# The casts of the activations' fourth combination, kept behind the last early Silu on ScalarE

## The chip, the cores and the metric

The kernel runs on one core of one Trainium2 chip. A core has five engines with an instruction queue each: TensorE (PE in the profile; its weight loads are shown as PEld), VectorE (DVE), ScalarE (ACT), GpSimd (POOL) and SyncE (SP), whose queue here issues most transfers to the 16 DMA engines. Every engine runs its queue in order, and the queues wait for each other. The metric is the device time of one execution in microseconds (us).

## The reference

The reference is a trunk of two layers on 1024 tokens of width 1024, in float32. A layer is a token mixer (latent attention in the first, differential attention in the second) and a SwiGLU feed-forward block, each followed by a layer norm on the residual sum. The change lies in the feed-forward block:

```python
D_FF = -(-8 * D_MODEL // (3 * 256)) * 256        # 2816

def _swiglu(x, w_gu, w_down):
    gate, up = jnp.split(x @ w_gu, 2, axis=-1)
    return (jax.nn.silu(gate) * up) @ w_down
...
        h = _layernorm(ALPHA * h + mix, ln_mix_g[i], ln_mix_b[i])
        h = _layernorm(ALPHA * h + _swiglu(h, ffn_w_gu[i], ffn_w_down[i]), ln_ffn_g[i], ln_ffn_b[i])
```

## The kernel before, in words

**Products.** Every float32 operand is split into a high part, a cast to fp32r on ScalarE (`A.copy`, in the profile CAST), and a low part, the rest, subtracted on VectorE or GpSimd. A product is three matmuls: high by high, high by low, low by high. The helper `split` (line 521) does this for all operands, so L521 stands for casts and low parts of many tiles; the tile's name tells them apart (t4h and t4l are the high and low part of t4; op_g and op_gp are split weights).

**The feed-forward block** (function `ffn`, called once per layer; I call the calls the first and the second block). The hidden width is 22 columns of 128, handled in the order `order`, n = 0 to 21. The two matmuls of gate and up with x are done by a Strassen-like scheme on 2 x 2 blocks: seven products per n instead of eight, named "1" to "7". Products "1" and "2" use the activations as they are (xh, xl) and accumulate into a bank `ga`; "5" and "3" use the combinations t1 and b22 and accumulate into `gc`; "6", "7" and "4" use t2, t3 and t4 and accumulate into `gb`. A product in the up-projection is twelve matmuls at line 565. The combinations of the activations are sums and differences of four blocks r11, r12, r21, r22 (tile xr), made in place on VectorE (lines 738 and 759) and split by `part`. The fourth combination, t4, is r21 - r22, with r22 already replaced by the second combination; its four casts write the tile t4h, four subtractions t4l.

**Early gates.** For n = 0 to 5 (`npre` = 6) products "1" and "2" are done ahead, while the last rows of the mixer are still on their way (`gates(0)`, `gates(2)`, `gates(4)`, two columns each). ScalarE copies the first result to the tile pg (line 626) and applies Silu to the second (line 628), into the same tile. `gates(2)` and `gates(4)` then store pg to HBM (line 704, tile pg_dr), as the buffer is wanted: all tiles made by `big_tile` share five buffers, and the raw weights gr of a later column, loaded at line 574, go where pg was. pg_dr is loaded back into tmp when n comes up (line 671).

**The main stream.** `stream` lists the products in the order of use, and `prepare` makes the weights' combinations (lines 596, 600, 602 and 606 on VectorE, on the tile gr) and splits them four products ahead. `consume` issues the twelve matmuls and then reads the bank on VectorE: after "6" at line 648, after "7" at line 652, after "4" at line 659. As "6", "7" and "4" of one n share a bank, the matmuls of "7" wait for line 648 and those of "4" for line 652. Two banks are there for gb, and TensorE takes n = 0 and n = 1 in turns.

**Order of work.** The order on each engine is written at build time by the tile framework's scheduler, from program order, priorities and modelled times. What the author wants otherwise is fixed by hand: `behind(i, j)` keeps instruction i behind instruction j; on one engine this is an order in its queue, with no semaphore. `part` takes such instructions as `after`, the first for the cast, the second for the low part. `newest` is a dictionary that remembers the latest instruction of some kind.

```python
        def part(key, k, src, eng, after=()):
            for i, j in zip(split([t[:, k] for t in xs[key]], src[:, k], eng), after):
                behind(i, j)
...
        gates(4)
...
        second("t3", r11, r22, r11, V, held)
        for k in range(4):
            part("t4", k, r21, V)
```

Of the kernel before, what the change touches and what calls it, by code (L numbers as in the profile page):

```python
# [11 lines left out]
AF = mybir.ActivationFunctionType  # L12
# [30 lines left out]
def trunk(  # L43
# [33 lines left out]
    V, A, G, T = nc.vector, nc.scalar, nc.gpsimd, nc.tensor  # L77
# [36 lines left out]
    def ps_s(name):  # L114
        return ps.tile([P, 512], F32, tag="s", bufs=ps_bufs[0], name=name)

    def ps_m(name):
        return ps.tile([P, 512], F32, tag="m", bufs=ps_bufs[1], name=name)
# [17 lines left out]
    newest = {}  # L136
# [43 lines left out]
    def behind(i, j):  # L180

        tc.add_manual_dep(
            i, j.name,
            mybir.DependencyInfo(mybir.DependencyClass.NoSync, mybir.DependencyReason.DATA),
            reason="kept in program order",
        )
# [162 lines left out]
    class OutProj:  # L349
# [73 lines left out]
        def split(self, tb, hs, o):  # L423
            oh, ol = (t[:, hs] for t in self.oh[tb])
            i = A.activation(oh, o, AF.Copy, scale=self.scale)
            j = V.scalar_tensor_tensor(ol, o, self.scale, f32(oh), ALU.mult, ALU.subtract)
            if tb in LAST_ORDER[2:4] and hs.start == 0:
                behind(i.ins, newest["hi"])
                behind(j.ins, newest["lo"])
# [107 lines left out]
    def ffn(side, xo, xst, pending, layer, x_src, x_dst, lng, lnb, next_x):  # L537
# [14 lines left out]
        r, tmp, ops, acc, hp, pg = {}, {}, {}, {}, {}, {}  # L552
        pg_dr = dr.tile([npre // 2, P, 4, 512], F32, name=f"pg_dr{layer}")

        def p1g0(n):


            t, i = (tmp[n], 2) if n in tmp and n > 1 else (pg[n // 2], 2 * (n % 2))
            return t[:, i], t[:, i + 1]

        def product(o, w, x, first):
            for k in range(4):
                kc = slice(k * P, (k + 1) * P)
                for a, b in ((0, 0), (0, 1), (1, 0)):
                    T.matmul(  # L565
                        o, w[:, a, kc], x[b][:, k, :], start=(first and k == 0 and (a, b) == (0, 0)),
                        stop=(k == 3 and a == 1), skip_group_check=True,
                    )
# [45 lines left out]
        def consume(n, pr):  # L614


            w, nm_ = ops.pop((n, pr)), f"{layer}_{n}"
            if pr in "12":
                if pr == "1":
                    acc[n, "a"] = ps_s(f"ga{nm_}")  # L620
                    if n >= npre:
                        new_tmp(n)
                product(acc[n, "a"], w, xo["12".index(pr), 0], pr == "1")
                p1, g0 = p1g0(n)
                if pr == "1":
                    A.copy(p1, acc[n, "a"])
                else:
                    A.activation(g0, acc[n, "a"], AF.Silu)
                return
            if pr in "53":  # L630
                if pr == "5" or n < 2:
                    acc[n, "c"] = c = (ps_s if n == 1 else ps_t)(f"gc{nm_}{pr}")
                    acc.setdefault((n, "cs"), []).append(c)
                product(acc[n, "c"], w, xs["t1" if pr == "5" else "b22"], pr == "5" or n < 2)
                if n < 2:
                    return
            else:
                if pr == "6":
                    acc[n, "b"] = ps_m(f"gb{nm_}")
                    if n < npre:  # L640
                        new_tmp(n)
                product(acc[n, "b"], w, xs[{"6": "t2", "7": "t3", "4": "t4"}[pr]], pr == "6")
            u2, u3 = tmp[n][:, 0], tmp[n][:, 1]
            p1, g0 = p1g0(n)
            if n == NFF - 1 and pr in "57":
                V.tensor_tensor(u3, p1 if pr == "5" else u3, acc[n, "c" if pr == "5" else "b"], ALU.add)
            elif pr == "6":
                V.tensor_tensor(u2, p1, acc[n, "b"], ALU.add)
                for c in acc[n, "cs"] if n < 2 else ():
                    V.tensor_tensor(u2, u2, c, ALU.add)  # L650
            elif pr == "7":
                V.tensor_tensor(u3, p1, acc[n, "b"], ALU.add)  # L652
                if n < 2:
                    V.tensor_tensor(u3, u3, acc[n, "cs"][0], ALU.add)
            elif pr == "5":
                V.tensor_tensor(u3, u3, acc[n, "c"], ALU.add)
            elif pr == "4":
                if n < NFF - 1:
                    V.tensor_tensor(p1, p1, acc[n, "b"], ALU.add)
            else:  # L660
                V.tensor_tensor(u2, u2, acc[n, "c"], ALU.add)  # L661
            if pr == ("4" if n < 2 else "3") and n < NFF - 1:
                activations(n, u2, u3, p1, g0)

        def new_tmp(n):
            if n == NFF - 1:
                tmp[n] = big_tile(f"tmp{layer}_{n}", F32).rearrange("p a (b c) -> p (a b) c", b=2)
                return
            tmp[n] = pool_a.tile([P, 4, 512], F32, tag="ra", name=f"tmp{layer}_{n}", bufs=2)
            if 1 < n < npre:  # L670
                nc.sync.dma_start(tmp[n][:, 2:4], pg_dr[n // 2][:, 2 * (n % 2):2 * (n % 2) + 2])

        def activations(n, u2, u3, p1, g0, after=()):
            j, kh = n // 2, n % 2
            i = A.activation(u2, u2, AF.Silu).ins  # L675
            for k in after[:1]:
                behind(i, k)
            if n == NFF - 1:
                i = V.tensor_tensor(p1, p1, acc[n, "b"], ALU.add).ins
                behind(i, after[1])  # L680
            if kh == 0:
                hp[j] = big_tile(f"hp{layer}_{j}", F32).rearrange("p a (b c) -> p (a b) c", b=2)

            i = V.tensor_tensor(hp[j][:, kh], g0, p1, ALU.mult).ins
            for k in after[1:]:
                behind(i, k)
            V.tensor_tensor(hp[j][:, 3 - kh], u2, u3, ALU.mult)
            if kh:
                h11, h12, h22, h21 = (hp[j][:, i] for i in range(4))
                t = big_tile(f"sh{layer}_{j}", F32).rearrange("p a (b c) -> p (a b) c", b=2)  # L690
                G.tensor_tensor(t[:, 0], h21, h22, ALU.add)
                G.tensor_tensor(t[:, 1], t[:, 0], h11, ALU.subtract)
                G.tensor_tensor(t[:, 2], h11, h21, ALU.subtract)
                G.tensor_tensor(t[:, 3], h12, t[:, 1], ALU.subtract)
                d = h_dr[j // 4][:, :, j % 4, :].rearrange("s p c -> p s c")
                nc.sync.dma_start(d[:, 0:3], hp[j][:, 0:3])
                nc.sync.dma_start(d[:, 3:7], t)

        def gates(n):
            for pr in "12":  # L700
                for i in (n, n + 1):
                    consume(i, pr)
            if n:
                nc.sync.dma_start(pg_dr[n // 2], pg[n // 2])
# [13 lines left out]
        r11, r12, r21, r22 = (xo["r", k, t] for k, t in ((0, 0), (0, 1), (1, 0), (1, 1)))  # L718
# [6 lines left out]
# [3 lines that stand above are left out]
# [31 lines left out]
            V.tensor_tensor(r21[:, k], r21[:, k], r22[:, k], ALU.subtract)  # L759
        second("t3", r11, r22, r11, V, held)  # L760
        for k in range(4):
            part("t4", k, r21, V)
        for i, u in enumerate(stream):
            if i + ahead < len(stream):
                prepare(*stream[i + ahead])
            consume(*u)
# [609 lines left out]
    xo, stacks = x_pools("m0", "right")  # L1376
    pending = out_proj("left", w_o_a, o_dr[0], x, xs_dr[0], ln_mix_g[0], ln_mix_b[0], xo)
    xT, rest, normed = ffn("left", xo, stacks, pending, 0, xs_dr[0], xs_dr[1], ln_ffn_g[0], ln_ffn_b[0], next_x)


# [186 lines left out]
    pending = proj[0].rest(ln_mix_g[1], ln_mix_b[1], xo)  # L1567
    banks("ps4", PS_BUFS)
    ffn("right", xo, stacks, pending, 1, xs_dr[2], out, ln_ffn_g[1], ln_ffn_b[1], None)
    ps_stack.close()  # L1570

# [87 lines left out]
```

## Time and profile before

| what | value |
|---|---|
| device time, median of 3 runs | 2265.44 us (2265.01 to 2267.45) |
| span of the profiled execution, first to last instruction | 2269.7 us |
| TensorE busy | 2238.7 us (99% of the span), 10850 matmuls |
| VectorE busy | 1593.1 us (70%) |
| ScalarE busy | 1007.1 us (44%) |
| GpSimd busy | 886.3 us (39%) |
| granted TensorE clock, mean | 0.997 of full speed |
| transfers | 289.25 MB, 127 GB/s on average |

How to read it: the profile is one execution, taken by the hardware profiler. Its span is 4.3 us longer than the median of the timed runs; no other time is given for the profiled execution, so differences are worked out on the span and taken over to the median. A busy engine is one with an instruction under way. The granted clock is the share of full speed that TensorE was given. The first feed-forward block's up-projections run from about 447 us to 868 us of the span, the second's from about 1626 us to 2052 us.

### The profile page before, as it was taken

How to read it: one execution, taken by the hardware profiler on the slowest of the kernel's cores; microseconds unless marked ns; L12 is line 12 of the kernel's file. 1: busy time of each engine (PE TensorE's matmuls, PEld its weight loads, DVE VectorE, ACT ScalarE, POOL GpSimd, SP SyncE). 2: the span in 40 equal slices, each digit the busy share in tenths (PEclk: the TensorE clock that was granted, in tenths of full speed). 3: DMA queues.
4: the chain of work that ended last, by engine and by line, in shares of the span. 5: the costliest groups of instructions: out<-in, count | busy, mean ns of one | idle time of the engine just before them, and what ended most of it. 6: DMA issues, size and time to landing. Idle time of an engine off the chain costs nothing.

```text
span 2269.7 us, 30075 instructions
## 1 busy us (share of the span) xinstructions
PE 2238.7 (99%) x10850; PEld 1883.5 (83%) x10850; DVE 1593.1 (70%) x2944; ACT 1007.1 (44%) x2077; POOL 886.3 (39%) x711
## 2 busy tenths in 40 slices
PE   9999999999999999999999999999999999999998
PEld 9888897878888888887888888877778888888886
DVE  6677774596656667778578777676586666568778
ACT  4455563352333334445466656555442332334444
POOL 2243451104544445555333435321014444446552
PEclk9999999999999999999999999999999999999999
DMA  6121335334324138454311212153334323247544
GB/s 207 41 95 59 121 98 186 116 145 148 139 70 139 70 114 335 177 199 153 112 43 33 61 35 64 42 209 114 137 132 150 108 83 126 82 150 269 204 171 159
DMA packets 104420, 289.25 MB, mean 127 GB/s; under 512 B 8656, under 2 KB 32080, under 8 KB 93776
## 3 DMA queue, kind: packets, MB, share of 16 engines
q1 hardware_dynamic: 100272, 277.90, 35.0%
q0 software_dynamic: 4000, 9.44, 1.5%
q8 instruction: 85, 1.39, 0.2%
q14 instruction: 63, 0.52, 0.1%
HBM read 205.78 MB, written 77.33 MB: 125 GB/s over the span
## 4 chain that ended last, share of the span: by engine, by line
PE 46%; DVE 5%; issue 1%; DMA 1%; ACT 1%; POOL 1%; POOLq 0%; DVEq 0%; SPq 0%; ACTq 0%
PE gb L565 8%; PE gc L565 5%; PE dw L871 4%; PE ga L565 4%; PE zp_a L440 3%; PE dx L871 3%; PE s_b L239 3%; PE bp L168 2%; PE bp L170 2%; PE bp L169 2%; PE bv L1409 2%; PE dv L871 1%; PE dy L871 1%; PE o_b L274 1%; PE pt_b L173 1%
## 5 line engine op out<-in xcount | busy, mean ns | idle before, releaser
L521 ACT CAST op_g<-gr 128x512 fp32r<-128x512 f32 x240 | 147.5, 622 | 403.5 <-PE gb L565 225.4
L521 POOL TENSOR_TENSOR op_g<-gr,op_g 128x512 fp32r<-128x512 f32 x104 | 146.1, 1410 | 303.4 <-DVE tmp L661 160.0
L521 DVE TENSOR_TENSOR op_h<-rh,op_h 128x512 fp32r<-128x512 f32 x154 | 164.0, 1090 | 58.8 <-ACT op_h L521 58.7
L565 PE MATMUL ga<-xh_m,op_g 128*128 128x512 f32 x512 | 168.0, 389 | 0.0
L871 PE MATMUL dw<-op_w_t,op_h 128*128 128x512 f32 x660 | 153.1, 391 | 1.8 <-DVE op_h L521 1.8
L521 ACT CAST op_h<-rh 128x512 fp32r<-128x512 f32 x154 | 92.3, 619 | 139.9 <-DMA rh<-h_dr 42.8
L871 PEld LDWEIGHTS dw<-op_w_t,op_h 128*128 128x128 f32 x660 | 123.2, 188 | 28.3 <-DVE op_h L521 2.8
L245 ACT ACTIVATE l_b<-l_b,mx_b 128x256 f32<-128x256 f32 (+7 forms) x128 | 99.5, 777 | 73.5 <-DVE mx_b L242 70.4
L521 POOL TENSOR_TENSOR op_w_t<-tt,op_w_t 128x512 fp32r<-128x512 f32 x66 | 98.2, 1490 | 81.2 <-ACT op_w_t L521 81.2
L565 PE MATMUL gb<-t3h_f,op_g 128*128 128x512 f32 x352 | 117.0, 394 | 3.6 <-ACT tmp L675 2.9
L1462 POOL TENSOR_SCALAR l_b<-l_b,r_b,cst 128x128 f32<-128x128 f32 (+3 forms) x64 | 52.5, 821 | 174.2 <-DVE r_b L247 152.9
L871 PE MATMUL dx<-op_w_b,op_h 128*128 128x512 f32 x528 | 120.3, 389 | 0.0
L565 PE MATMUL gb<-t4h_f,op_g 128*128 128x512 f32 x352 | 115.7, 390 | 0.8 <-DVE tmp L652 0.8
L871 PEld LDWEIGHTS dx<-op_w_b,op_h 128*128 128x128 f32 x528 | 99.1, 188 | 20.6
L521 DVE TENSOR_TENSOR op_g<-gr,op_g 128x512 fp32r<-128x512 f32 x136 | 110.3, 811 | 8.4 <-ACT op_g L521 8.1
L565 PE MATMUL gc<-b22h_f,op_g 128*128 128x512 f32 x352 | 115.5, 389 | 0.0
L565 PE MATMUL gc<-t1h_f,op_g 128*128 128x512 f32 x352 | 115.5, 389 | 0.0
L565 PE MATMUL gb<-t2h_f,op_g 128*128 128x512 f32 x352 | 115.1, 389 | 0.0
L521 POOL TENSOR_TENSOR op_g<-s,op_g 128x512 fp32r<-128x512 f32 x40 | 54.3, 1358 | 151.8 <-ACT op_g L521 151.7
L565 PEld LDWEIGHTS ga<-xh_m,op_g 128*128 128x128 f32 x512 | 96.1, 188 | 19.9
L168 PE MATMUL bp<-xT_f,h_wb 128*128 128x512 f32 x256 | 103.2, 403 | 0.2
L169 PE MATMUL bp<-xT_f,h_wb 128*128 128x512 f32 x256 | 101.9, 398 | 0.0
(389 smaller groups left out, 6567.9 us busy)
## 6 DMA issues: line engine op xcount, KB each, us to landing
gr<-in_w_gu SPq DMA_DIRECT2D x44, 1024.0 KB, 6.9
rh<-h_dr SPq DMA_DIRECT2D x28, 1024.0 KB, 5.0
h_dr<-sh SPq DMA_DIRECT2D x22, 1024.0 KB, 4.9
h_dr<-hp SPq DMA_DIRECT2D x22, 768.0 KB, 4.0
tt<-in_w_dn SPq DMA_DIRECT2D x22, 512.0 KB, 8.2
rh<-h_dr SPq DMA_DIRECT2D x14, 768.0 KB, 4.4
z<-xs_dr SPq DMA_DIRECT2D x16, 512.0 KB, 11.3
rw_b<-in_w_dn SPq DMA_DIRECT2D x8, 1024.0 KB, 8.1
```

What stands on the lines that cost most here:

```text
L168: T.matmul(ps_out, lh, rh, start=(i == 0), stop=False)
L169: T.matmul(ps_out, lh, rl, start=False, stop=False)
L170: T.matmul(ps_out, ll, rh, start=False, stop=(i == n - 1))
L173: T.transpose(ps_out, in_, ident)
L239: T.matmul(s[:, :w], lh, rh[:, ks], start=(j == 0), stop=(j == len(q_pass) - 1))
L245: newest["exp"] = A.activation(l[:, :n], l[:, :n], AF.Exp, bias=mx, scale=-1.0, accum_out=sm).ins
L440: T.matmul(m, a[:, h, :], self.wo[h][w][:, c], start=(start and h == heads[0] and a is oh and w == 0), stop=(stop and h == heads[-1] and a ...
L521: return A.copy(hi, src).ins, eng.tensor_tensor(lo, src, f32(hi), ALU.subtract).ins
L565: T.matmul(o, w[:, a, kc], x[b][:, k, :], start=(first and k == 0 and (a, b) == (0, 0)), stop=(k == 3 and a == 1), skip_group_check=True,)
L871: i = T.matmul(o, h[:, a, c], w[:, b_], start=(first and (a, b_) == (0, 0)), stop=(last and a == 1), skip_group_check=True,).ins
L1409: T.matmul(m, xT[0][hf][:, k, c], w[k], start=(k == 0), stop=False, skip_group_check=True)
L1462: G.tensor_scalar(l1[:, :n], l1[:, :n], r1, nlam, ALU.mult, ALU.mult)
```

## The change

In `consume` the Silu of every early or later gate is remembered as `newest["silu"]`. Where the fourth combination is split, the four casts on ScalarE are kept behind the Silu that is the newest at that point. At that point in the program the last Silu issued is the one in `gates(4)`, for n = 5. The low parts on VectorE get no order of their own (`after` has one entry). The same code runs in both blocks.

```diff
@@ -625,7 +625,7 @@
                 if pr == "1":
                     A.copy(p1, acc[n, "a"])
                 else:
-                    A.activation(g0, acc[n, "a"], AF.Silu)
+                    newest["silu"] = A.activation(g0, acc[n, "a"], AF.Silu).ins
                 return
             if pr in "53":
                 if pr == "5" or n < 2:
@@ -759,7 +759,7 @@
             V.tensor_tensor(r21[:, k], r21[:, k], r22[:, k], ALU.subtract)
         second("t3", r11, r22, r11, V, held)
         for k in range(4):
-            part("t4", k, r21, V)
+            part("t4", k, r21, V, (newest["silu"],))
         for i, u in enumerate(stream):
             if i + ahead < len(stream):
                 prepare(*stream[i + ahead])
```

## Rows read from the trace of the kernel before

**Rows 1.** The page: part 1, busy us by engine; part 4, the chain's shares
```profile
PE 2238.7 (99%) x10850; PEld 1883.5 (83%) x10850; DVE 1593.1 (70%) x2944; ACT 1007.1 (44%) x2077; POOL 886.3 (39%) x711
...
PE 46%; DVE 5%; issue 1%; DMA 1%; ACT 1%; POOL 1%; POOLq 0%; DVEq 0%; SPq 0%; ACTq 0%
```

**Rows 2.** Waits of TensorE, whole span: total us, times, longest us
```profile
PE gb L565 <- ACT tmp L675: 2.9, 1, 2.9
...
PE gb L565 <- DVE tmp L652: 0.8, 1, 0.8
...
PE gb L565 <- ACT op_g L521: 0.7, 1, 0.7
```

**Rows 3.** The chain in order of time, second block: start us, us, what
```profile
1668.51 4.09 DMA pg_dr<-pg
...
1672.66 6.18 DMA gr<-in_w_gu
...
1678.93 0.69 DVE gr L596
```

**Rows 4.** Stretches: length, busy us by engine (instructions), PEclk, DMA share, GB/s
```profile
500.10:503.00 2.90, 2.90 (x12) 2.12 (x12) 2.90 (x4) 0.63 (x1) 1.29 (x1) 1.00 0.00 0
1664.00:1666.00 2.00, 2.00 (x11) 1.65 (x10) 2.00 (x4) 0.20 (x1) 0.00 (x0) 1.00 0.00 0
1668.00:1670.00 2.00, 2.00 (x11) 1.65 (x10) 2.00 (x5) 2.00 (x4) 0.00 (x0) 1.00 0.97 410
1682.70:1687.20 4.50, 4.43 (x13) 3.53 (x14) 4.19 (x6) 1.12 (x2) 1.28 (x1) 0.62 0.00 0
```

**Rows 5.** Timeline of TensorE, second block: start us, us, line, what, [idle before]
```profile
1663.18 0.39 PE L565 MATMUL ga<-xh_m,op_gp 128*128 128x512 f32 x1
...
1671.34 0.39 PE L565 MATMUL gb<-t2h_f,op_g 128*128 128x512 f32 x1
...
1682.77 0.47 PE L565 MATMUL gb<-t3h_f,op_g 128*128 128x512 f32 x1 [2.93 <-ACT tmp L675]
...
1687.18 0.40 PE L565 MATMUL gb<-t4h_f,op_g 128*128 128x512 f32 x1
...
1689.92 0.39 PE L565 MATMUL gc<-t1h_f,op_g 128*128 128x512 f32 x1
```

**Rows 6.** Timeline of VectorE, second block
```profile
1676.05 0.68 DVE L648 TENSOR_TENSOR tmp<-pg,gb 128x512 f32<-128x512 f32 x1
1678.93 0.69 DVE L596 TENSOR_TENSOR gr<-gr 128x512 f32<-128x512 f32 x1 [2.20 <-DMA gr<-in_w_gu]
...
1681.95 0.67 DVE L648 TENSOR_TENSOR tmp<-pg,gb 128x512 f32<-128x512 f32 x1
...
1685.02 0.67 DVE L652 TENSOR_TENSOR tmp<-pg,gb 128x512 f32<-128x512 f32 x1
```

**Rows 7.** Timeline of ScalarE, first block
```profile
483.12 0.60 ACT L628 ACTIVATE pg<-ga 128x512 f32<-128x512 f32 x1 [1.59 <-PE ga L565]
...
484.61 2.19 ACT L521 CAST t4h_f<-xr_m 128x512 fp32r<-128x512 f32 x4 [0.37 <-DVE t3l_f L521]
```

**Rows 8.** Timeline of ScalarE, second block
```profile
1665.81 2.19 ACT L521 CAST t4h_f<-xr_m 128x512 fp32r<-128x512 f32 x4 [2.75 <-DVE t3l_f L521]
1667.90 0.58 ACT L628 ACTIVATE pg<-ga 128x512 f32<-128x512 f32 x1
```

**Rows 9.** Waits of SP's queue, 1655 to 1675 us
```profile
SPq L704 <- ACT pg L628: 2.9, 1, 2.9
```

**Rows 10.** Timeline of SP's queue, 1664 to 1668 us
```profile
1665.20 0.33 SPq L574 DMA_DIRECT2D gr<-in_w_gu  x1
```

**Rows 11.** The tile gr, 1650 to 1690 us: its loads, from issue to landing
```profile
DMA to landing us min/median/max: 4.8/4.9/6.2
```

**Rows 12.** Timeline of TensorE, first block
```profile
491.08 0.39 PE L565 MATMUL gb<-t2h_f,op_g 128*128 128x512 f32 x1
...
503.83 0.50 PE L565 MATMUL gb<-t4h_f,op_g 128*128 128x512 f32 x1 [0.76 <-DVE tmp L652]
```

## The prediction, made before the changed kernel was run

> **What bounds the kernel now.** I read the page first: TensorE is busy for 99% of the span, and the chain that ended last is TensorE where it is not short bits of VectorE, ScalarE and transfers [rows 1]. So an edit that adds no matmul can only give back or take TensorE's waits. I then listed those waits over the whole execution: the up-projections (gb) lose 2.9 us once, 0.8 us once and 0.7 us once [rows 2]. The 2.9 us lie in the second feed-forward block, the two small ones in the first, as the timelines show. Next I followed the chain back from the 2.93 us. It reads, backwards: a matmul at 1682.77, VectorE's add on gr at 1678.93, the load of gr issued at 1672.66, the store of pg at 1668.51, which waits for pg [rows 3]. What writes pg is the Silu of the last early gate, n = 5, on ScalarE. The load of raw weights for n = 4 (I call it gr4) goes into the buffer that the stored gates leave, so it can't be issued before the store has landed.
>
> The table of stretches shows a second loss at the same place: behind the wait the granted clock averages 0.62 from 1682.7 to 1687.2, so part of it ran at 1.2 instead of 2.4 GHz [rows 4]. The twelve matmuls of that product stretch from 1682.77 to 1687.18, 4.41 us; the next twelve, at full clock, stretch from 1687.18 to 1689.92, 2.74 us [rows 5]. The clock costs 1.67 us; wait and clock together cost 2.93 + 1.67 = 4.60 us. That is the most that the change can give back there, 0.20% of the time.
>
> One name in the waits is not the true one. The profile puts the 2.93 us down to a Silu on tmp. The product needs the bank that VectorE's L648 reads, at 1681.95 for 0.67 us [rows 6]: its end, 1682.62, is 0.15 us ahead of the matmul. So TensorE starts again at the end of L648 plus 0.15 us.
>
> **The change part by part.** Nothing is computed anew and no semaphore is added: `behind` only fixes an order on one engine. In the first block the Silu of n = 5 starts at 483.12 and the four casts t4h at 484.61 [rows 7]; the order asked for is already there, and I cost the edit at nothing. In the second block the casts start at 1665.81 and the Silu at 1667.90 [rows 8]; here they change places.
>
> What the Silu gains. Its last matmul starts at 1663.18 and takes 0.39 us, so its input stands at 1663.57 [rows 5]. ScalarE is idle for the 2.75 us ahead of 1665.81, so from 1663.06, for the casts wait for a VectorE result [rows 8]. The Silu (0.58 us) fits into that gap, over by about 1664.2 instead of 1668.48, and the casts still start at 1665.81: putting them behind costs nothing as long as VectorE is what they wait for. If that cover were gone they would be late by at most the Silu's 0.58 us, with their first reader on TensorE at 1687.18.
>
> What the store gains. It doesn't go at 1664.2: the queue of SP has a gr load at 1665.20 ahead of it, and from there the store waited 2.9 us for the Silu [rows 9, 10]. With the Silu early it follows the load's issue of 0.33 us, at about 1665.6 instead of 1668.51. Landing: before, it took 4.1 us (1668.51 to 1672.6) [rows 3]; alone it would land at 1669.7. But it now lies wholly beside the gr load of 1665.20. Two transfers of 1 MB are 2.1 MB; at the 410 GB/s that the DMA engines moved while both were under way, from 1668 to 1670 [rows 4], they need 5.1 us, and no data moved before 1666 (0 GB/s from 1664 [rows 4]), so both are over near 1671.2. I take 1671.2, since the overlap is complete.
>
> What gr4 gains. It is issued at once, and the loads in this stretch took 4.8 to 6.2 us to land [rows 11]; this very load took 6.2 [rows 3]. So it lands from 1671.2 + 4.8 = 1676.0 to 1677.5, middle 1676.8, instead of 1678.9. With the lone store's 1669.7 the early end is 1674.5.
>
> What VectorE gains. Its add L596 waited 2.20 us for gr4; the instruction ahead of it ends at 1676.73 [rows 6]. With gr4 at 1676.8 it starts near 1676.85, 2.1 us earlier; with the bounds above 2.2 and 1.4 us earlier. L648 and L652 stand behind it in the same queue and move by the same amount, since everything between them was back to back.
>
> What TensorE gains. L648 ends at 1680.52 and the product starts at 1680.67, after 0.83 us of idling. In the first block a wait of 0.7 us, ended near 500, was followed by a granted clock of 1.00 [rows 2, 4], here one of 2.93 us by 0.62; 0.83 is near the first, so I take no loss of clock. The product then ends at about 1683.6 (2.74 us, and 0.2 us for the last to drain). The next one, on t4, waits for L652, at 1685.02 for 0.67 us before: 1685.69 - 2.1 + 0.15 = 1683.74 against 1687.18, a gain of 3.44 us. The first block gives a second reading, since the same code has its Silu early there: from the first matmul on t2 to the first on t4 it takes 503.83 - 491.08 = 12.75 us [rows 12], the second block 1687.18 - 1671.34 = 15.84 us [rows 5], which is 3.09 us more. I take 3.2, between the two. Nothing later takes it back by the rows: the list has no other wait on gb in the second block, and in the first, with its start as tight, none but the two small ones.
>
> The Trainium skill's page DMA: Bandwidth & Descriptors (section Anatomy of one DMA, SWDGE (gpsimd) path) prices a transfer, measured there on the software-issued path, at a fixed 2.0 us and its bytes over 436 GB/s, an estimate of 4.4 us for this store against the trace's 4.1. For 2.1 MB in flight at once it gives 6.8 us, so that the store would land at 1672.0, 0.6 us early, and the sum would be 0.6 us to some 2 us instead of 3.2; this speaks against the change and stands beside the first rival.
>
> **Sum.** The profiled execution spans 2269.7 us, 4.3 us above the median of 2265.44 us; 3.2 us off the span is 2266.5, and off the median 2262.2 us, 0.14% less. A difference of 0.2%, 4.5 us, is about what a measurement of this kernel can tell from none, so this forecast falls under "same".
>
> **The rivals.**
> The DMA engines give it back (0.20). Store and gr load could take, together, as long as they did when 3 us apart, 1665.2 to 1672.6: then gr4 isn't earlier and the time stays at 2265.4. Half way, gr4 lands 0.7 us earlier, TensorE still idles for 2.2 us, the clock still falls, and the time is 2264.7. For it: the DMA engines are busy for 0.97 of the time at 1668 to 1670 [rows 4]. Against it: at the rate of that stretch both are through by 1671.2. That page of the Trainium skill leans to this rival.
>
> More comes back than forecast (0.13). If the order around the place also puts L648 ahead of the add that waits for gr4, as both are free to be, TensorE never waits for that load; all 4.60 us come back, 2260.8 us. For it: L648's own input is the product on t2, which precedes the t3 product that is then waiting. Against it: the add came first in the order of before [rows 6].
>
> Slower (0.13). The order on VectorE is written anew where the casts move. If the four low parts of t4, which follow the casts, come to stand behind L596, they add 4 x 0.60 = 2.4 us (the spacing of the instructions there [rows 6]) between it and L648. L648 would start at 1676.85 + 3.02 + 2.4 = 1682.3, or 1682.9 with gr4 at 1677.5, against 1681.95: 0.3 to 1.0 us later, 2265.7 to 2266.4 us. It decides only if gr4 lands after 1676.5. A longer idle may also hold the clock low for longer; doubled, that is 1.7 us more, 2268.1. A changed order in the 580 us that follow, which no row bounds, I count here and in the case above, with 0.05 or so each beyond 0.2%.
>
> The change does nothing (0.04): if the Silu's place in the second block stayed as it is, 2265.4.
>
> **How the numbers follow.** The forecast has 0.50: 2261.3 (with 2.2 us earlier and the larger reading, plus 0.5 for the spread of runs) to 2263.6 (1.4 us earlier, 2.7 us gained, and the same spread). Range: below it reaches under 2260.8 by the spread of the runs, to 2259.8; above, to 2267.0, past the slower case's 2266.4. Faster by over 0.2% needs less than 2260.9: most of the second rival, 0.12. Slower by over 0.2% needs more than 2270.0: 0.07. Same: 0.81.
>
> **What would show it.** Right: in the second block the Silu of n = 5 near 1663.6 and the casts still near 1665.8; the store issued near 1665.6 and landing near 1671; the add on gr4 with under 1 us of idling; TensorE's wait on gb under 1.5 us and no stretch under a clock of 1.00 behind it. The first block unchanged. Wrong: a store that is issued early and lands no earlier (the DMA rival), a VectorE order in which t4's low parts precede L648, or a TensorE wait in a place where there was none.

## The result: slower by 0.14%, outside the range and on the other side

| | median us | lowest to highest, runs |
|---|---|---|
| before | 2266.28 | 2263.12 to 2267.96, 21 |
| after | 2269.66 | 2264.58 to 2272.34, 21 |
| after / before | 1.0014, interval 1.0009 to 1.0020 | |

The forecast was 2262.2 us, 0.14% faster, within 2259.8 to 2267.0. The kernel lost about as much as it was to gain. The profiled execution of after spans 2266.2 us, and its time is 2267.92 us, one of the shorter of its runs; this matters below. A span lies some 1.7 us under its time, so the profile of before that the prediction was made from, with its span of 2269.7 us, stands for some 2271.4 us (an estimate), above every one of these 21 runs of before.

In order of instructions two things changed, both in the second block: the Silu of n = 5 stands ahead of the four casts t4h on ScalarE, and one subtraction of n = 2 (L602) went two places forward on VectorE. TensorE, GpSimd and SP keep their orders, and the first block is as it was, as forecast.

The page and TensorE's waits, after (as [rows 1, 2]; waits: total us, times, longest):

```profile
PE 2237.3 (99%) x10850; PEld 1881.0 (83%) x10850; DVE 1589.8 (70%) x2944; ACT 1007.4 (44%) x2077; POOL 885.6 (39%) x711
```

```profile
PE gb L565 <- ACT tmp L675: 1.7, 1, 1.7
```

The wait is 1.7 us, where [rows 2] had 2.9; the two small ones, 0.8 and 0.7, are unchanged. By these lines alone the change would have helped. The chain in order of time (start us, us, what) says otherwise, beside [rows 3]:

```profile
1662.70 0.61 ACT pg L628
1663.31 0.01 issue
1663.32 7.60 DMA pg_dr<-pg
...
1670.99 5.05 DMA gr<-in_w_gu
...
1676.13 0.69 DVE gr L596
...
1679.76 0.64 ACT tmp L675
1680.40 0.07 issue
1680.47 6.06 PE gb L565 x24
```

The store of pg now takes 7.60 us; it took 4.09 in [rows 3]. Timelines of ScalarE, SP and VectorE, after (as [rows 8, 10, 6]):

```profile
1662.70 0.60 ACT L628 ACTIVATE pg<-ga 128x512 f32<-128x512 f32 x1 [1.61 <-PE ga L565]
1663.19 2.17 ACT L521 CAST t4h_f<-xr_m 128x512 fp32r<-128x512 f32 x4
```

```profile
1655.62 6.83 SPq L574 DMA_DIRECT2D gr<-in_w_gu  x2
1663.32 0.33 SPq L704 DMA_DIRECT2D pg_dr<-pg  x1
1670.99 0.33 SPq L574 DMA_DIRECT2D gr<-in_w_gu  x1
```

```profile
1668.49 0.69 DVE L596 TENSOR_TENSOR gr<-gr 128x512 f32<-128x512 f32 x1 [0.38 <-DMA gr<-in_w_gu]
...
1676.13 0.69 DVE L596 TENSOR_TENSOR gr<-gr 128x512 f32<-128x512 f32 x1 [2.01 <-DMA gr<-in_w_gu]
...
1679.65 0.68 DVE L648 TENSOR_TENSOR tmp<-pg,gb 128x512 f32<-128x512 f32 x1
```

The second of the two gr issues (the load for n = 3) ends at 1655.62 + 6.83 = 1662.45, so it was issued at 1662.12, and the store 1.2 us behind it. The load lands late too: VectorE waits 0.38 us for it at 1668.49, and it is the longest of the landings of gr in this stretch (as [rows 11], where the longest was that of gr4):

```profile
DMA to landing us min/median/max: 4.7/5.0/6.4
```

TensorE after (as [rows 5]), and four stretches (columns as [rows 4]):

```profile
1670.43 0.39 PE L565 MATMUL gb<-t2h_f,op_g 128*128 128x512 f32 x1
...
1680.47 0.47 PE L565 MATMUL gb<-t3h_f,op_g 128*128 128x512 f32 x1 [1.72 <-ACT tmp L675]
...
1683.47 0.50 PE L565 MATMUL gb<-t4h_f,op_g 128*128 128x512 f32 x1
```

```profile
1664.00:1666.00 2.00, 2.00 (x11) 1.65 (x10) 2.00 (x4) 2.00 (x5) 0.00 (x0) 1.00 1.02 344
1666.00:1668.00 2.00, 2.00 (x11) 1.65 (x10) 2.00 (x4) 0.49 (x2) 0.00 (x0) 1.00 0.87 344
1668.00:1670.00 2.00, 2.00 (x11) 1.65 (x10) 1.62 (x4) 0.54 (x1) 0.00 (x0) 1.00 0.64 270
1680.40:1684.90 4.50, 4.43 (x18) 3.36 (x19) 4.50 (x7) 1.35 (x3) 1.29 (x1) 1.00 0.00 0
```

Behind the wait the clock is 1.00 here. From 1664 to 1668, where load and store both run, the rate is 344 GB/s, less than the 410 of before from 1668 to 1670; in that last stretch it is 270 here with the DMA engines busy for 0.64: the store is still under way, and they are no longer full.

### The profile page after: what moved, and what is told of

Its sections match the earlier page's. It is cut to its first block, busy times and chain, and to the rows that moved or that the text cites. A ratio compares the mean times of both kernels' runs of the same rounds, so it can differ in the third digit from the quotient of the medians.

```text
span 2266.2 us, 30075 instructions
## 1 busy us (share of the span) xinstructions
PE 2237.3 (99%) x10850; PEld 1881.0 (83%) x10850; DVE 1589.8 (70%) x2944; ACT 1007.4 (44%) x2077; POOL 885.6 (39%) x711
## 4 chain that ended last, share of the span: by engine, by line
PE 48%; DVE 3%; DMA 2%; issue 1%; ACT 1%; POOL 0%; SPq 0%; POOLq 0%; DVEq 0%; ACTq 0%
PE gb L565 8%; PE ga L565 5%; PE gc L565 5%; PE dw L871 4%; PE zp_a L440 3%; PE s_b L239 3%; PE dx L871 3%; PE bp L168 3%; PE bp L170 3%; PE bp L169 3%; PE bv L1409 2%; PE dv L871 1%; PE dy L871 1%; PE o_b L274 1%; PE pt_b L173 1%
```

## The experiments

Theory: the store, issued early, runs nearly wholly beside the load for n = 3; it lands no sooner than before, both take longer than they would apart, and the load for n = 4 (gr4) and TensorE's wait behind it follow. Rivals: the new order on VectorE costs the time; the new order on ScalarE itself does; or nothing was lost and both kernels only spread. All ratios are to before, run beside each kernel on the same chip.

To compare executions that drift by a few us, this table counts from the first matmul on t2 in the second block (worked out from the timelines: each start less that matmul's). gr4 goes out within 0.1 us of the store's landing. "Clock" is the granted one in the 4.5 us behind the wait.

| run | gr n=3 issued | store issued, us to landing | add on gr4 starts | TensorE waits | clock | first matmul on t4 |
|---|---|---|---|---|---|---|
| before, first profile | -6.14 | -2.83, 4.1 | 7.59 | 2.93 | 0.62 | 15.84 |
| e1 (before) | -7.49 | -4.18, 4.1 | 5.14 | 1.31 | 1.00 | 12.63 |
| e13d (before) | -8.05 | -4.74, 4.1 | 4.53 | 0.18, ahead of t4 | 1.00 | 11.55 |
| after | -8.31 | -7.11, 7.6 | 5.70 | 1.72 | 1.00 | 13.04 |
| e2 (after) | -8.33 | -7.11, 7.6 | 5.75 | 1.77 | 1.00 | 13.09 |
| e8 (after) | -8.13 | -7.11, 8.4 | 6.94 | 3.10 | 1.00 | 14.42 |
| e13a (after) | -7.65 | -7.11, 8.4 | 7.76 | 3.27 | 0.50 | 16.85 |
| e13b (after) | -7.28 | -6.83, 8.5 | 7.07 | 3.10 | 0.50 | 16.68 |
| e13c (after) | -7.90 | -7.11, 8.3 | 7.63 | 3.14 | 0.62 | 15.88 |
| e3 | -7.86 | -7.11, 8.2 | 7.33 | 3.10 | 0.62 | 15.84 |
| e4 | -6.65 | -7.11, 4.8 | 3.99 | none | | 10.88 |
| e5 | -7.35 | -4.53, 4.5 | 5.22 | 1.31 | 1.00 | 12.63 |

**Both kernels again.** e1 is the kernel before unchanged, e2 the kernel after unchanged, five rounds each.

> The kernel before, unchanged, for a second profile of it and as a check of the comparison. Theory A (the profile of before showed an unusual execution; as a rule gr4 lands earlier there): time within 0.1% of before, span near 2264.5 us, TensorE's wait on gb in the second block 1.0 to 2.0 us and no low clock behind it. Theory B (the profile of before was typical, and the loss of the changed kernel lies in another stage): a wait of 2.9 us with 3.4 us of half clock again, span near 2264.5 us with some other stage 5 us shorter than in the first profile.

> The changed kernel, unchanged, for a second profile. Theory A: 1.0010 to 1.0020 of before; the store takes 7 to 8 us beside the load of gr for n = 3, gr4 lands no earlier than in the new profile of before, and where the span is above 2267 us TensorE's wait on gb is above 2 us with 3.4 us or more of half clock behind it. Theory B: the second block as in the first profile of the changed kernel (wait 1.7 us, clock 1.00), and a loss of 3 us elsewhere.

e1: 2267.45 us, ratio 1.0000 (0.9991 to 1.0009). e2: 2272.42 us, 1.0015 (1.0006 to 1.0025). The loss is there again. More telling is e1's profile. Its SP and TensorE timelines:

```profile
1657.43 7.65 SPq L574 DMA_DIRECT2D gr<-in_w_gu  x2
1668.06 0.33 SPq L704 DMA_DIRECT2D pg_dr<-pg  x1
1672.21 0.33 SPq L574 DMA_DIRECT2D gr<-in_w_gu  x1
```

```profile
1681.87 0.47 PE L565 MATMUL gb<-t3h_f,op_g 128*128 128x512 f32 x1 [1.31 <-ACT tmp L675]
...
1684.87 0.50 PE L565 MATMUL gb<-t4h_f,op_g 128*128 128x512 f32 x1
```

Here before waits 1.31 us, not 2.93, and the clock behind it is full; it stores 3.3 us behind the load's issue, and the store takes 4.1 us. The 4.60 us that the prediction set out to give back are mostly not there in this execution.

**Single executions of each.** e8 and e13a to e13c are the kernel after, e13d the kernel before, each a single execution with its profile. They were made because the first two profiles of after show 0.4 us more waiting than e1, too little for 3.4 us.

> The changed kernel once more, for a third profile. Collision theory: store 7 to 8 us, VectorE's wait for gr4 2 to 3 us, TensorE's wait 1.7 to 3.2 us; with the clock at one half behind it if the wait is near 3 us, and then a span near 2269.5 us.

> The kernel after, one more execution. Three profiles of it so far had a wait for gb of 1.7, 1.8 and 3.1 us, at full clock, and their times (2267.1 to 2267.9) lie below the median of its timed runs (2269.7 and 2272.4). If the loss of 0.15% is this wait, often with a stretch at 1.2 GHz behind it, some execution of these three has a wait of 2.5 to 3.3 us and a granted clock near 0.6 in the 4.5 us behind it, at a time above 2269. If the loss lies elsewhere, a time above 2269 comes with a wait under 2 us and a clock of 1.00 there.

> The kernel after once more: a time above 2269 goes with a wait over 2.5 us and the lower clock behind it, a time below 2268 with one under 2 us or a full clock. If the loss lies elsewhere, the time doesn't go with the wait.

> The kernel after, the last of three: the same two readings as for the two before it, a time above 2269 with a wait over 2.5 us and the lower clock behind it, or with neither.

> The kernel before, a third execution: a wait for gb of 1.3 us in the second block, full clock, 2265 to 2268 us. If its first profile, with 2.93 us and the lower clock behind, was the usual case: 2.5 to 3.1 us again, above 2269.

Times: e8 2267.12, e13a 2273.29, e13b 2271.36, e13c 2268.76 us, against 2267.03 for the run of before beside the e13 ones, and e13d 2270.54. The chain, TensorE and the stretches of e13a:

```profile
1664.03 0.61 ACT pg L628
1664.64 0.02 issue
1664.65 8.44 DMA pg_dr<-pg
...
1673.16 6.27 DMA gr<-in_w_gu
```

```profile
1683.36 0.77 PE L565 MATMUL gb<-t3h_f,op_g 128*128 128x512 f32 x1 [3.27 <-ACT tmp L675]
...
1688.61 0.63 PE L565 MATMUL gb<-t4h_f,op_g 128*128 128x512 f32 x1
```

```profile
1683.30:1687.80 4.50, 4.44 (x11) 3.51 (x12) 4.19 (x6) 1.11 (x2) 1.28 (x1) 0.50 0.00 0
1687.80:1690.60 2.80, 2.80 (x10) 2.22 (x9) 1.75 (x3) 0.62 (x1) 0.00 (x0) 0.71 0.01 3
```

In e8 a wait nearly as long left the clock alone (TensorE's timeline and the stretch behind it; the last line is TensorE in e13d):

```profile
1679.46 0.47 PE L565 MATMUL gb<-t3h_f,op_g 128*128 128x512 f32 x1 [3.10 <-ACT tmp L675]
```

```profile
1679.40:1683.90 4.50, 4.43 (x18) 3.41 (x19) 4.50 (x7) 1.36 (x3) 1.29 (x1) 1.00 0.00 0
```

```profile
1686.10 0.50 PE L565 MATMUL gb<-t4h_f,op_g 128*128 128x512 f32 x1 [0.18 <-DVE tmp L652]
```

So in six executions of after the wait is 1.72 to 3.27 us, in four of them over 3, and in three of these four TensorE runs at 1.2 GHz behind it. In three of before it is 2.93, 1.31 and 0.18. The medians of the last column are 15.15 (half way between 14.42 and 15.88) and 12.63: 2.5 of the 3.4 us that the timed runs lost. The time doesn't follow the wait strictly: e13c has 3.14 us and the low clock at only 2268.76, since its first matmul on t2 came at 1668.52, 3.7 us sooner than e1's; e13d has no wait over 0.2 us in that place, where I expected 1.3, and took 2270.54: its t2 came 2.3 us later than e1's, 1.6 of them lost ahead of the product on dw that ends the first block.

By their whole times these nine executions even say the opposite: the median is 2270.5 us for before (with 2271.4 for the first profile) and 2268.3 for after. TensorE's timelines show where that arises. From the first matmul on t4 in the second block to the end of the span all nine take 582.5 to 583.1 us, and the first block's stretch from t2 to t4 takes 12.74 or 12.75 us. From the second block's first product to its first matmul on t2 they take 45.2 to 45.4 us. What else differs lies ahead of the second block, where both kernels have the same order on every engine; the first matmul on t2 comes at 1671.34 to 1674.55 in before and at 1668.03 to 1671.76 in after. So what these profiles show of the change lies in the stretch from t2 to t4 alone, and the rest of the span varies between executions by as much. Nine single times can't show the loss; the timed runs do.

The timed runs carry a sign of the lower clock too: the mean granted clock of an execution is 0.996 in 10 of the 33 runs of after (21 and e2's 12), each of them at 2269.2 us or more, and in 4 of 105 runs of before (e1's and those beside e1 to e12, without one of 2780 us).

**ScalarE's order alone.** e3 is the kernel after with VectorE's old order written out:

```diff
-                V.tensor_tensor(a12, a12, a11, ALU.subtract)
+                i = V.tensor_tensor(a12, a12, a11, ALU.subtract).ins; n != 2 or behind(i, newest["t4", 2][1])
...
-            for i, j in zip(split([t[:, k] for t in xs[key]], src[:, k], eng), after):
-                behind(i, j)
+            newest[key, k] = made = split([t[:, k] for t in xs[key]], src[:, k], eng)
+            [behind(i, j) for i, j in zip(made, after)]
```

> The Silu ahead of the casts on ScalarE, as in the changed kernel, but VectorE's queue pinned to the order of before (three low parts of t4 ahead of L602, one behind). Theory A, the early store costs the time: as the changed kernel, 1.0010 to 1.0020. Rival, the two places that L602 moved on VectorE cost it: as before, 0.9995 to 1.0005.

2271.48 us, 1.0016 (1.0007 to 1.0024): the whole loss. The order on VectorE is not its cause. Its chain and the stretch behind the wait:

```profile
1664.14 8.21 DMA pg_dr<-pg
...
1672.42 6.07 DMA gr<-in_w_gu
```

```profile
1682.60:1687.10 4.50, 4.42 (x13) 3.52 (x14) 4.21 (x6) 1.14 (x2) 1.28 (x1) 0.62 0.00 0
```

**The store held.** e5 is the kernel after, with this one store waiting for the fourth cast t4h (and L648 of n = 1 pinned in its place on VectorE, so that all orders stay those of after):

```diff
-            if n:
+            if n and (layer, n) != (1, 4):
                 nc.sync.dma_start(pg_dr[n // 2], pg[n // 2])
...
-            part("t4", k, r21, V, (newest["silu"],))
+            part("t4", k, r21, V, (newest["silu"],)); k < 3 or not layer or late_store(newest[layer, "t4", 3][0])
```

> The changed kernel, every queue in the same order, but the store of the last early gates in the second block waits until the fourth cast of t4 has ended on ScalarE, which is about when it went in the kernel before. Collision theory (the store, put on its way early, runs beside the load of gr for n = 3 and lands no sooner, while that load lands later): store 4 to 5 us instead of 7 to 8, TensorE's wait on gb 1.0 to 1.6 us, time 0.9993 to 1.0007 of before. Rival (the new order on ScalarE or VectorE costs the time, whenever the store goes): 1.0010 to 1.0020 as in the changed kernel.

2266.91 us, 1.0003 (0.9994 to 1.0011). Here `late_store` issues the same store, with a dependency on that cast. SP's timeline of e5:

```profile
1665.33 0.33 SPq L706 DMA_DIRECT2D pg_dr<-pg  x1
1669.92 0.33 SPq L574 DMA_DIRECT2D gr<-in_w_gu  x1
```

```profile
1679.49 0.47 PE L565 MATMUL gb<-t3h_f,op_g 128*128 128x512 f32 x1 [1.31 <-ACT tmp L675]
```

The Silu stays early and the casts stay behind it; only the store goes 2.3 to 2.6 us later and takes 4.5 us, gr4 goes out at 0.06 instead of 0.55 to 1.73, and TensorE's wait is 1.31 us, as in e1. A store issued later lands sooner: ScalarE's new order costs nothing that shows by itself, the store that it sets free does.

**The store first.** e4 and e12 (the same kernel on another chip) let the store go ahead of the load for n = 3 in SP's queue; VectorE's order shifts a little with it:

```diff
-            nc.sync.dma_start(r[n], w_gu[layer, order[n]])
+            i = nc.sync.dma_start(r[n], w_gu[layer, order[n]]).ins; n != 3 or behind(i, newest["store"])
...
-                nc.sync.dma_start(pg_dr[n // 2], pg[n // 2])
+                newest["store"] = nc.sync.dma_start(pg_dr[n // 2], pg[n // 2]).ins
```

> The changed kernel with the load of gr for n = 3 kept behind the store on SP's queue; some additions on VectorE change places with it. Theory A: the store now lands 5 to 6 us after its issue near 1663.4, gr4 some 2 us earlier than in the changed kernel, the load for n = 3 1.5 to 3 us later; TensorE's wait on gb falls under 1 us if VectorE doesn't wait for n = 3, and the time is 0.9985 to 0.9995 of before. Theory B: as the changed kernel, 1.0010 to 1.0020.

> The same kernel as the run with 0.9991 [0.9983, 1.0000], on the chip of the other three. If the store ahead of the load beats the kernel before by removing its wait of 1.3 us: 0.9988 to 0.9995. If that ratio was within the spread of the runs: 0.9996 to 1.0004.

e4: 2266.23 us, 0.9991 (0.9983 to 1.0000). e12: 2265.54 us, 0.9992 (0.9983 to 1.0001). SP's timeline and the landings of gr, e4:

```profile
1662.31 0.33 SPq L704 DMA_DIRECT2D pg_dr<-pg  x1
1662.77 4.75 SPq L574 DMA_DIRECT2D gr<-in_w_gu  x2
```

```profile
DMA to landing us min/median/max: 4.9/5.0/6.9
```

The two transfers overlap as fully as in after, 0.46 us apart, but now the store, first in line, takes 4.8 us and the load behind it 6.9. So it is not the overlap alone that costs. The load is slowed either way: 6.9 us here, 6.4 to 6.9 in the six executions of after, 4.8 or 4.9 in the three of before. The store is slowed much only when it is second: 7.6 to 8.5 us there, 4.8 here, 4.1 in before. In after gr4 hangs on the store; here what pays is the load for n = 3 alone, for which VectorE's add waits only 0.74 us. gr4 is issued at -2.23, and TensorE doesn't wait. Each ratio's interval reaches 1.00, so the gain in time is likely but small; that the wait is gone is plain.

e6 puts the same edit into the kernel before, where the Silu is still late.

> The kernel before, casts ahead of the Silu, with the load of gr for n = 3 kept behind the store; additions on VectorE change places with it. If the gain of the run with the store first came from SP's order alone: 0.998 to 0.9995 of before here too. If the early Silu is what makes room for it: the store goes near 4 us ahead of the first t2 matmul, the load for n = 3 lands some 3 us later than before, VectorE waits for it, and the time is 1.000 to 1.002.

2267.45 us, 1.0003 (0.9995 to 1.0012). The load now stands behind a store that waits for the late Silu, is issued at -4.38 instead of -7.49, and its add starts at 2.43 instead of -1.59; TensorE waits 1.45 us. Ahead of the load, the store takes TensorE's wait away only with the Silu early. In time that would be a use for the change that its own form hasn't got, but the intervals of e4, e12 and e6 overlap.

**The store in halves.** e7 is the kernel after with the half of n = 4 stored as soon as its own Silu is done.

```diff
-                nc.sync.dma_start(pg_dr[n // 2], pg[n // 2])
+                for c in ((slice(0, 2), slice(2, 4)) if (layer, n) == (1, 4) else (slice(0, 4),)): nc.sync.dma_start(pg_dr[n // 2][:, c], pg[n // 2][:, c])
```

> The changed kernel with that store cut in two: the half of n = 4 follows its own Silu, 2 us ahead of the load of gr for n = 3, the half of n = 5 follows the last Silu. Collision theory: less lies beside the load, the second half lands 4.5 to 5.5 us after its issue, gr4 3 to 4 us ahead of the changed kernel, no wait on gb over 0.8 us, time 0.9985 to 0.9995 of before. Rival (order on the engines costs the time): not under 1.000.

2267.78 us, 1.0002 (0.9993 to 1.0011). That misses the forecast, and by the time it is the rival's figure. The halves go at -9.83 and -7.11; the second takes 6.5 us, where I expected 4.5 to 5.5, and gr4 goes out at -0.29, at least 0.8 us sooner than in after. But VectorE's order came out otherwise (the add on gr4 stands ahead of L648 of n = 0 as well), and TensorE waits 0.53 + 1.17 us. With the order changed too, this run decides nothing.

**The add behind the read.** Wherever TensorE waited over 1.2 us for gb in the second block so far, L648 of n = 1 stood behind the add on gr4 in VectorE's queue, while its own inputs were ready. e9 (before), e10 (after) and e11 (e4) turn these two round, in both blocks. The scheduler moves some other instructions of VectorE with them, ahead of this place too, so it isn't this exchange alone:

```diff
-                if n < 2:
-                    behind(i, fourth[1])
+                if n < 2 or n == 4:
+                    behind(i, fourth[1] if n < 2 else newest["read"])
...
-                V.tensor_tensor(u2, p1, acc[n, "b"], ALU.add)
+                i = V.tensor_tensor(u2, p1, acc[n, "b"], ALU.add).ins; newest["read" if n == 1 else n] = i
```

> The kernel before, with the addition of n=4 (L596) kept behind the read of n=1's accumulators (L648) in VectorE's queue, in both blocks. Chain theory (TensorE waits in the second block only because L648 of n=1 stands behind an addition that waits for a load): the wait for gb goes from 1.3 us to at most 0.8 us there, the first matmul of t4 starts 11 to 12 us after the first of t2 instead of 12.6, and the time falls by 0.5 to 1.5 us (ratio 0.9993 to 0.9998). Rival (the late addition holds up n=4's own Silu and lows, and TensorE waits for these in the next group): the wait moves to n=4's group, ratio 0.9998 to 1.0005.

> The kernel after, with the same order on VectorE. Chain theory: the store and the load still collide (store 7 to 8.5 us, the load of n=4 issued as it lands), but the wait for gb goes from 1.7-3.1 us to at most 0.8 us, no stretch at 1.2 GHz behind it, and the loss of 0.15% is gone: ratio to before 0.9993 to 1.0003. Rival (n=4's own group then waits for its late addition): a wait of 1 to 3 us a group later, ratio 1.0008 to 1.0018 as the change itself.

> The change with the store of the second pair ahead of n=3's load on SyncE's queue, as in the run with 0.9991, and with the addition of n=4 behind the read of n=1. Chain theory: there was no wait left in that place to take away, so 0.9986 to 0.9994, no better than the run without the second edit by more than 0.0003. Rival (the addition's place costs or gains by itself): below 0.9984 or above 0.9997.

| run | median us | ratio | wait for gb, second block | first matmul on t4 |
|---|---|---|---|---|
| e9, from before | 2264.46 | 0.9983 (0.9974 to 0.9992) | none | 11.01 |
| e10, from after | 2264.61 | 0.9985 (0.9977 to 0.9994) | 0.89 | 12.07 |
| e11, from e4 | 2264.41 | 0.9984 (0.9975 to 0.9993) | none | 10.89 |

VectorE's timeline of e9: the read first, and the add meets data that has landed.

```profile
1678.50 0.68 DVE L648 TENSOR_TENSOR tmp<-pg,gb 128x512 f32<-128x512 f32 x1
1679.09 0.69 DVE L596 TENSOR_TENSOR gr<-gr 128x512 f32<-128x512 f32 x1
```

VectorE's and TensorE's timelines of e10:

```profile
1670.46 0.69 DVE L596 TENSOR_TENSOR gr<-gr 128x512 f32<-128x512 f32 x1 [0.81 <-DMA gr<-in_w_gu]
...
1675.41 0.68 DVE L648 TENSOR_TENSOR tmp<-pg,gb 128x512 f32<-128x512 f32 x1
```

```profile
1676.15 0.50 PE L565 MATMUL gb<-t3h_f,op_g 128*128 128x512 f32 x1 [0.89 <-DVE tmp L648]
```

All three gained more than I expected. In e10 store and load still collide (store 8.8 us, issued at -5.56, the load for n = 4 at 3.62). The wait of 1.7 to 3.3 us is gone; the 0.89 that is left is a little over the 0.8 expected, and stands behind another add, the one on the load for n = 3, which is late too. The kernel is still as fast as the others: with the add on gr4 out of the way the change costs nothing that shows in the time. That supports the chain: most of what the late gr4 loses, it loses through that add.

Part of the gain comes from the first block, where the same order takes away its two waits for gb (0.8 and 0.7 us): from t2 to t4 it takes 10.88 us there in all three, 1.9 less than the 12.75 of before. e9's profile gives 1.4 us of it back at 977 us, where VectorE waits for down-projection weights and TensorE 1.73 us for VectorE; e11 has this wait too. It needn't be the edit's price: e13d and e7 have it without the edit, and e10, with it, hasn't. The rest, e9 against e1 in the second block, is 12.63 - 11.01 = 1.6 us. The 3.5 us of the medians are more than the 2.3 us between the two profiles' spans; e9's profiled execution was the slowest of its eleven, and no other of them has a profile. e11 lies 0.0008 below e12, more than the 0.0003 expected and at the edge of the rival's figure, that the place of the add gains by itself; the edit is made in the first block as well, so this doesn't tell apart whether the early store still gives anything. These three are the fastest versions run, 0.15 to 0.17% under before.

## Why the prediction was wrong

In its steps' order, counted from the first matmul on t2 as in the table (1671.34 in the profile that the prediction used):

| step | forecast | measured, six executions of after |
|---|---|---|
| first block | unchanged | unchanged |
| Silu of n = 5 | -7.7, into the gap | -7.73 |
| casts t4h | -5.53, not later | -7.24 to -6.67, not later |
| store issued | -5.74 | -7.11 to -6.83 |
| store lands | -0.14 | 0.48 to 1.66 |
| store takes | 5.6 us | 7.6 to 8.5 us |
| gr4's load takes | 5.6 us (4.8 to 6.2) | 5.0 to 6.3 us |
| add on gr4 | 5.5 | 5.70 to 7.76 |
| TensorE's wait | 0.83 us, full clock | 1.72 to 3.27 us, in three of six with the low clock |
| first matmul on t4 | 12.40 | 13.04 to 16.85 |

**The step that failed first is what the change had to win.** "Wait and clock together cost 4.60 us" held for the one execution profiled, and I subtracted the 3.2 us from the median of other executions. Two more profiles of before show 1.31 and 0.18 us at full clock. Against 12.63, the middle one of the three, my own 12.40 would have been a gain of 0.2 us, so no change that can be measured; three executions can't say how often each occurs. The signs were in the rows: a span 4.3 us above the median, and the first block's 12.75 us [rows 12], which I took for a second reading of the gain, where it is near what the second block itself took in e1.

**The second is the term for the store's landing, which was mis-sized, and it gives the sign.** "Two transfers of 1 MB are 2.1 MB; at the 410 GB/s ... they need 5.1 us" took a rate from a stretch in which the two overlapped in part, for two that overlap nearly wholly; there the rate was 344 GB/s and then 270. In the profile of after both are through at 1670.92, 8.8 us after the load's issue, where I had 6.0 (1665.2 to 1671.2). That is longer than the pair needs when its issues lie 3.3 us apart (7.4 us in e1), and the store, second in line, bears most of it: gr4 goes out behind it later than in e1 (0.55 to 1.73 against -0.03) though the store is issued 2.6 to 2.9 us sooner. The early issue was right; its worth had the wrong sign. The prediction's sentence on the Trainium skill's page DMA: Bandwidth & Descriptors (section Anatomy of one DMA, SWDGE (gpsimd) path) gave an estimate of 6.8 us for the pair; the trace goes the same way and further, to 8.8.

**From there the chain ran as written.** gr4 goes out as the store lands, VectorE's add waits for it, L648 and TensorE follow (add to L648 3.0 to 3.7 us, 3.0 forecast), and behind three of the four waits over 3 us the clock is low. The store isn't all of the longer waits: gr4's own load took 6.3 us in e13a and e13c and 5.0 to 5.5 in the other four, and in e8 and e13b the add took 1.35 and 1.21 us instead of 0.69. That the store's time decides and not the Silu, the casts or VectorE's order as such is shown by e3 and e5, and e10 agrees.

**The rivals.** "The DMA engines give it back" named the right mechanism and stopped at zero: it held the time unchanged where gr4 isn't earlier, and had no term for gr4 becoming later, since before was taken at its worst. "Slower" put the loss on t4's low parts behind L596; they stayed ahead of it. Its other part, a clock held low for longer, did come in e13a and e13b: the mean granted clock is 0.51 over the 6.9 us from 1682.50 in e13a. "More comes back" (L648 ahead of the add) didn't happen by itself; made to happen in e9 to e11, it gives 2264.4 to 2264.6 us beside 2267.93 for before.

What stays open: why the store is slowed so much more behind the load than the load behind the store; why it takes 7.6 us in two executions, where it is issued 1.2 us behind the load, and 8.3 to 8.5 in the four where it is 0.45 to 1.0 us; why gr4's load takes 5.0 us in one execution and 6.3 in another; and why the clock fell behind one wait of 3.10 us and not behind another.

## What to carry to other kernels

A wait in one profiled execution is not yet a loss of the kernel: put the profile's span beside the timed median, and look at the same place in a second execution, before counting the wait as something to win. A transfer issued earlier may run into another one: ask which of the two is then first in line, how long each takes in that order, and what hangs on the second. And where a wait for data stands ahead of an instruction that needs none of it, turning the two round in the queue may be worth more than bringing the data sooner.

## What the runs showed of the hardware

What two transfers of 1 MB cost together depended on their order. With the store first and the load 0.46 us behind, they took 4.8 and 6.9 us, and both were through 7.3 us after the first issue (e4). With the load first and the store 0.45 to 1.2 us behind, the load took 6.4 to 6.9 us and the store 7.6 to 8.5, and both were through after 8.8 to 9.4 us (the six executions of after). With the store 3.3 us behind they took 4.9 and 4.1 us, 7.4 us in all (e1). Holding the store back by 2.3 to 2.6 us made it land 0.5 us or more sooner (e5).

The granted clock after a wait isn't set by the wait's length alone in what can be seen here: behind 3.10 us it stayed at 1.00 in e8, and was 0.50 in e13b and 0.62 in e3, behind waits of the same 3.10 us; behind 1.31 to 1.77 us it never fell. In e13a the low clock lasted past 1687.80, with 0.50 in the first 4.5 us and 0.71 in the next 2.8.
